# The last feed-forward projection as seven products of halves for sixteen of its twenty-two row tiles

## The chip, the cores and the metric

The kernel runs on one core of a Trainium2 chip. The metric is the device time of one execution in microseconds (us). A profile gives the span from the first to the last instruction of one execution; the execution's time also holds what lies around the span.

## What is computed

Two layers on 512 tokens of width 1024: dilated attention, a gated feed-forward block (SwiGLU), an mLSTM mixer, a second SwiGLU, and a final RMS norm. The change touches the second half of the last SwiGLU and the norm behind it:

```python
def swiglu(xn, w_in, w_out):
    gu = xn @ w_in
    return (jax.nn.silu(gu[..., :D_FF]) * gu[..., D_FF:]) @ w_out      # D_FF = 2816

h = h + swiglu(rms_norm(h, ffn_norm[i]), ffn_w_in[i], ffn_w_out[i])    # i = 1 is the last
return rms_norm(h, final_norm)
```

So the last projection multiplies the hidden values (512 tokens x 2816) by `w_out` (2816 x 1024), adds the residual `h`, and each token's row of 1024 is normalised and written out. All is float32.

## The kernel before

**How float32 is multiplied.** Each operand is split into a rounded value (`_h`, type fp32r, made on ScalarE, ACT) and a residue (`_l`, made on VectorE, DVE, as source minus rounded value). Each float32 product is then three matmuls (`SPLITS`): high by high, high by low, low by high. For a chunk of weights the two instructions are L208 (ACT) and L209 (DVE), both 128x1024.

**Layer 1 of the feed-forward block** is `ffn_in` (its hidden values) and then the block at L1577 on (its projection). `ffn_in` makes the hidden values in eleven tiles `hid[0]` to `hid[10]`, each two row tiles of 128 of the 2816, by 512 tokens. The first three come from `plain`. The other eight already come as seven products of halves each (`products`, L1186, matmuls 256 wide, accumulators `c`, `p` and `u`). While the last of them (named `f1j20`, since it starts at row tile 20) runs, `split_hidden` begins to split the hidden values into `f1hh` (L1254, ACT) and `f1hl` (L1257, DVE), 128x1024 each, in the order of the tiles.

**The projection before.** For each half `n` of the 1024 output features, the loop runs over eleven chunks of `w_out`, each two row tiles by 512 features (`fw_w`, 512 KB, loaded through SyncE's queue, SP, into three buffers and split into `fw_h` and `fw_l`). A chunk is multiplied with the four blocks of 128 tokens (`tb`), 2 x 3 matmuls of 512 features for each (L1620). In the first half, eight groups of four transposes (`hT`, L305) bring `h` from its feature-major form into token-major tiles `ht` on the way. The last three chunks of a half are held back and multiplied block by block, so that one block after the other ends:

```python
            tiles = [(tb, tb, slice(0, 512)) for tb in range(TB)]
            if n == 1:
                tiles[-1:] = [(TB - 1, TB - 1, slice(0, 256)), (TB, TB - 1, slice(256, 512))]
```

The last block of the second half is thus made in two pieces of 256 features, and its matmuls are 256 wide throughout. Behind each block DVE adds the accumulator to `ht` (L1636), ACT squares it with a running sum (`fsq`, L1639), GpSimd (POOL) multiplies it by the gains `gbc` (L1644), and behind the second half of a block come the inverse root (L1648 to L1655), the scaling of both halves (L1657 on ACT, L1659 on DVE) and two output DMAs (L1658, L1660).

**What sets the order.** The code records operations, and a scheduler places each engine's instructions by their dependences and by the order of recording, so an engine's queue is not the order of the source. A tile is one of a few buffers under a tag; the instruction that first writes it waits until the readers of the tile that held the buffer before are done.

Of the kernel before, what the change touches and what calls it, by code (L numbers as in the profile page):

```python
# [11 lines left out]
F32 = mybir.dt.float32  # L12
F32R = mybir.dt.float32r
# [58 lines left out]
def tile_hybrid_dilated_attn_mlstm(  # L72
# [272 lines left out]
    with ExitStack() as actx:  # L345
# [241 lines left out]
        class Values:  # L587
# [15 lines left out]
            def load(self, key, ch, to, add=False):  # L603
                view = to.rearrange("p (k n) -> p k n", k=2)
                if add:
                    nc.gpsimd.dma_start(view, self.source(key, ch), accum_op=ALU.add)
                else:
                    nc.sync.dma_start(view, self.source(key, ch))
# [416 lines left out]
    PLAIN = 6  # L1025
    AHEAD = 2

    def ffn_in(layer, fp, pair, rbc, hook, following):

# [231 lines left out]
        for n, (j, i) in enumerate(todo):  # L1263
            prepare(n + AHEAD)
            if i == 0:
                steps_of = products(j, prepared[j][1])
            steps_of[i]()
            if i % 2:
                advance()
            if n >= len(todo) - 3:  # L1270
                split_hidden()
        while len(parts[0]) < len(hid):
            split_hidden()
        return [[tiles[k // 2][:, k % 2] for k in range(FC)] for tiles in parts], out_weights
# [302 lines left out]
    with ExitStack() as fctx:  # L1577
        fp = pool(fctx, "ffn1")
        wo = ffn_w_out[1]

        def load(ch, n):
            src = wo[ch * 2 * P:(ch + 1) * 2 * P, n * 512:(n + 1) * 512].rearrange("(k p) n -> p k n", p=P)
            return split_weights(src, [P, 2, 512], "fw%d_%d" % (n, ch))
        a, ready = ffn_in(1, fp, pair, rbc, hook, lambda ch: load(ch, 0))
        gbc = fp.tile([P, D], F32, tag="t1", name="gbc")
        nc.gpsimd.dma_start(gbc, final_norm.unsqueeze(0).to_broadcast([P, D]))

        ht = [[None, None] for _ in range(TB)]
        ht_tiles = [fp.tile([P, 4, SEQ], F32, tag="w8", name="ht%d" % i, bufs=2) for i in range(2)]

        def residual(i):
            tb, n = i // 2, i % 2
            tp = ps.tile([P, 512], F32, tag="so"[i % 2], name="hT%d" % i, bufs=2)
            for k in range(4):
                transpose_into(tp, k, h[4 * n + k][:, tb * P:(tb + 1) * P])
            t = ht_tiles[i // 4][:, i % 4]
            nc.scalar.activation(t, tp, AF.Copy)
            ht[tb][n] = t
        NCH = FC // 2
        fss = fp.tile([P, TB, 3], F32, name="fss")  # L1600
        fpre, fv, fr, fa = (fp.tile([P, TB], F32, name="f" + n) for n in ("pre", "v", "r", "a"))
        nc.gpsimd.memset(fss, 0.0)
        nc.gpsimd.tensor_scalar(gbc, gbc, -0.5, None, op0=ALU.mult)
        tail = 3
        for n in range(2):
            acc = ([acc_tile("fin%d" % i) for i in range(3)] + [ps.tile([P, 512], F32, tag="t", name="fin3", bufs=1)]
                   if n == 0 else
                   [ps.tile([P, 512], F32, tag=tg, name="fin4", bufs=2) for tg in ("s", "s", "o", "o")]
                   + [acc_tile("fin5")])


            tiles = [(tb, tb, slice(0, 512)) for tb in range(TB)]
            if n == 1:
                tiles[-1:] = [(TB - 1, TB - 1, slice(0, 256)), (TB, TB - 1, slice(256, 512))]

            def mm(whl, ch, i, tb, cs):
                for k in range(2):
                    kk = 2 * ch + k
                    for a_, b_ in SPLITS:
                        nc.tensor.matmul(acc[i][:, cs], a[a_][kk][:, tb * P:(tb + 1) * P], whl[b_][:, k, cs],  # L1620
                                         start=(kk == 0 and (a_, b_) == SPLITS[0]),
                                         stop=(kk == FC - 1 and (a_, b_) == SPLITS[-1]))

            for ch in range(NCH - tail):
                whl = ready.pop(0) if ready else load(ch, n)
                for t in tiles:
                    mm(whl, ch, *t)
                if n == 0 and 1 <= ch <= TB:
                    residual(2 * ch - 2)
                    residual(2 * ch - 1)  # L1630
            last = [load(ch, n) for ch in range(NCH - tail, NCH)]
            for at, tb, cs in tiles:
                for i in range(tail):
                    mm(last[i], NCH - tail + i, at, tb, cs)
                t = ht[tb][n][:, cs]
                nc.vector.tensor_tensor(t, acc[at][:, cs], t, op=ALU.add)  # L1636
                junk = npl.tile([P, SEQ], F32, tag="sq", name="fsq", bufs=2)
                part = 0 if n == 0 else 1 if cs.stop < 512 else 2
                nc.scalar.activation(junk[:, cs], t, AF.Square, accum_out=fss[:, tb, part:part + 1])  # L1639
                if part == (1 if tb == TB - 1 else 0):  # L1640
                    nc.vector.tensor_tensor(fpre[:, tb:tb + 1], fss[:, tb, 0:1], fss[:, tb, 1:2], op=ALU.add)
                    nc.vector.tensor_scalar(fpre[:, tb:tb + 1], fpre[:, tb:tb + 1], 1.0 / D, EPS,
                                            op0=ALU.mult, op1=ALU.add)
                nc.gpsimd.tensor_tensor(t, t, gbc[:, n * 512 + cs.start:n * 512 + cs.stop], op=ALU.mult)  # L1644
                if n == 1 and cs.stop == 512:

                    v = fv[:, tb:tb + 1]
                    nc.vector.scalar_tensor_tensor(v, fss[:, tb, 2:3], 1.0 / D, fpre[:, tb:tb + 1],  # L1648
                                                   op0=ALU.mult, op1=ALU.add)
                    r = fr[:, tb:tb + 1]  # L1650
                    a2 = fa[:, tb:tb + 1]
                    nc.scalar.activation(r, v, AF.Sqrt)
                    nc.vector.reciprocal(r, r)
                    nc.vector.tensor_scalar(a2, r, v, r, op0=ALU.mult, op1=ALU.mult)
                    nc.vector.scalar_tensor_tensor(r, a2, -3.0, r, op0=ALU.add, op1=ALU.mult)  # L1655
                    t0, t1 = ht[tb]
                    nc.scalar.activation(t0, t0, AF.Copy, scale=r)  # L1657
                    nc.scalar.dma_start(out[tb * P:(tb + 1) * P, 0:512], t0)  # L1658
                    nc.vector.tensor_scalar(t1, t1, r, None, op0=ALU.mult)  # L1659
                    nc.sync.dma_start(out[tb * P:(tb + 1) * P, 512:1024], t1)  # L1660


# [22 lines left out]
```

## Time and profile before

| | us |
|---|---|
| median of three executions | 1433.47 (1430.98 to 1434.05) |
| the profiled execution's own time | 1431.08 |
| its span | 1428.8 |

The page gives busy time by engine, and windows of the span give it by stage. TensorE's matmul unit is PE, its weight loads are PEld. Matmuls overlap in the pipeline, so the duration of a row is longer than the distance between two starts; how much work a stage holds is read from the starts. POOL's DMAs go through a queue of their own (software), SP's and ACT's through the others.

### The profile page before, as it was taken

What the parts mean: (1) busy time and instruction counts of PE and PEld (TensorE: products, weight loads), DVE (VectorE), ACT (ScalarE), POOL (GpSimd) and SP (SyncE); (2) the same over time, 40 slices, a digit from 0 to 9 for tenths busy, and PEclk for the clock granted to TensorE, in tenths of its full rate; (3) what the DMA queues carried; (4) which work ended last, traced back from release to release, by engine and by line L of the source; (5) the groups of instructions that cost most, each with busy time, mean ns of one, the idle gap of its engine ahead of it and who ended that gap; (6) DMA issues with size and microseconds to landing.
All of it is one profiled execution on the core that took longest, in us unless ns stands there. A gap on an engine that the chain in (4) does not pass through costs nothing. (4 is left out here: it accounts for less than half of the span.)

```text
span 1428.8 us, 20252 instructions
## 1 busy us (share of the span) xinstructions
PE 1410.0 (99%) x7968; PEld 1234.9 (86%) x7968; DVE 988.5 (69%) x1697; ACT 621.3 (43%) x1027; POOL 78.1 (5%) x131
## 2 busy tenths in 40 slices
PE   9999999999999999999999999999999999999997
PEld 7788888888888888999988888798888899998886
DVE  7976685966676587777863359987759777786223
ACT  7245522324224443454542234785544344555222
POOL 1014010100001000000000010100000000000101
PEclk9999999999999999999999999999999999999998
DMA  9538353363525333332233333221233233313231
GB/s 297 144 86 210 96 167 121 99 211 98 176 89 165 108 95 111 119 118 80 70 111 97 103 91 89 75 75 50 84 102 101 93 118 119 105 59 119 74 118 59
DMA packets 132182, 160.74 MB, mean 112 GB/s; under 512 B 7092, under 2 KB 112884, under 8 KB 132088
## 3 DMA queue, kind: packets, MB, share of 16 engines
q1 hardware_dynamic: 123696, 135.75, 30.7%
q0 software_dynamic: 6736, 22.59, 6.1%
q8 instruction: 62, 1.02, 0.3%
q10 hardware_dynamic: 1656, 1.12, 0.2%
q14 instruction: 32, 0.26, 0.1%
HBM read 145.28 MB, written 12.06 MB: 110 GB/s over the span
## 5 line engine op out<-in xcount | busy, mean ns | idle before, releaser
L1620 PE MATMUL fin<-fw_h,f1hh 128*128 128x512 f32 (+1 forms) x198 | 72.8, 368 | 0.0
L1620 PE MATMUL fin<-fw_l,f1hh 128*128 128x512 f32 (+1 forms) x198 | 72.5, 366 | 0.0
L1620 PE MATMUL fin<-fw_h,f1hl 128*128 128x512 f32 (+1 forms) x198 | 72.4, 366 | 0.0
L209 DVE TENSOR_TENSOR fw_l<-fw_w,fw_h 128x1024 fp32r<-128x1024 f32 x22 | 27.0, 1233 | 65.5 <-ACT fw_h L208 65.5
L209 DVE TENSOR_TENSOR fo_k_l<-fo_k_w,fo_k_h 128x1024 fp32r<-128x1024 f32 (+1 forms) x24 | 27.2, 1133 | 62.0 <-ACT fo_k_h L208 62.0
L239 PE MATMUL fo<-f0hh,fo_k_h 128*128 128x512 f32 x176 | 68.5, 389 | 0.0
L239 PE MATMUL fo<-f0hl,fo_k_h 128*128 128x512 f32 x176 | 68.5, 389 | 0.0
L239 PE MATMUL fo<-f0hh,fo_k_l 128*128 128x512 f32 x176 | 68.5, 389 | 0.0
L208 ACT ACTIVATE fo_k_h<-fo_k_w 128x1024 fp32r<-128x1024 f32 (+1 forms) x24 | 23.7, 989 | 74.4 <-PE fo L239 74.4
L208 ACT ACTIVATE fw_h<-fw_w 128x1024 fp32r<-128x1024 f32 x22 | 23.3, 1059 | 67.8 <-PE fin L1620 67.8
L1620 PEld LDWEIGHTS fin<-fw_h,f1hl 128*128 128x128 f32 x198 | 37.3, 189 | 6.1
L1620 PEld LDWEIGHTS fin<-fw_l,f1hh 128*128 128x128 f32 x198 | 37.4, 189 | 6.0 <-DVE fw_l L209 0.2
L1620 PEld LDWEIGHTS fin<-fw_h,f1hh 128*128 128x128 f32 x198 | 37.4, 189 | 6.0
L239 PEld LDWEIGHTS fo<-f0hh,fo_k_h 128*128 128x128 f32 x176 | 33.0, 188 | 6.9
L239 PEld LDWEIGHTS fo<-f0hl,fo_k_h 128*128 128x128 f32 x176 | 33.0, 188 | 6.9
L239 PEld LDWEIGHTS fo<-f0hh,fo_k_l 128*128 128x128 f32 x176 | 33.0, 188 | 6.7
L239 PE MATMUL f1j<-n_h,f1j_h 128*128 128x512 f32 x96 | 37.5, 390 | 0.0
L239 PE MATMUL f0j<-n_h,f0j_h 128*128 128x512 f32 x96 | 37.5, 390 | 0.0
L239 PE MATMUL f0j<-n_h,f0j_l 128*128 128x512 f32 x96 | 37.4, 389 | 0.0
L239 PE MATMUL f1j<-n_h,f1j_l 128*128 128x512 f32 x96 | 37.4, 389 | 0.0
L239 PE MATMUL f0j<-n_l,f0j_h 128*128 128x512 f32 x96 | 37.3, 389 | 0.0
L239 PE MATMUL f1j<-n_l,f1j_h 128*128 128x512 f32 x96 | 37.3, 389 | 0.0
(2127 smaller groups left out, 4896.8 us busy)
## 6 DMA issues: line engine op xcount, KB each, us to landing
f0j_w<-in_ffn_w_in_dram SPq DMA_DIRECT2D x28, 512.0 KB, 4.8
f1j_w<-in_ffn_w_in_dram SPq DMA_DIRECT2D x28, 512.0 KB, 3.6
fw_w<-in_ffn_w_out_dram SPq DMA_DIRECT2D x22, 512.0 KB, 3.9
fo_k_w<-in_ffn_w_out_dram SPq DMA_DIRECT2D x20, 512.0 KB, 3.4
awo_k_w<-in_attn_w_out_dram SPq DMA_DIRECT2D x8, 512.0 KB, 4.5
mv_k_w<-in_mlstm_w_in_dram SPq DMA_DIRECT2D x8, 512.0 KB, 3.6
mqk_k_w<-in_mlstm_w_in_dram SPq DMA_DIRECT2D x8, 512.0 KB, 3.8
mo_k_w<-in_mlstm_w_in_dram SPq DMA_DIRECT2D x8, 512.0 KB, 3.6
```

The lines of the kernel that those rows point to most:

```text
L208: nc.scalar.activation(hi[:, :n], raw[:, :n], AF.Copy)
L209: nc.vector.tensor_tensor(lo[:, :n], raw[:, :n], hi[:, :n].bitcast(F32), op=ALU.subtract)
L239: nc.tensor.matmul(acc, whl[a][:, k, m * P:(m + 1) * P], pairs[b][kk], start=(kk == 0 and (a, b) == SPLITS[0]), stop=(kk == nk - 1 and (a, ...
L1620: nc.tensor.matmul(acc[i][:, cs], a[a_][kk][:, tb * P:(tb + 1) * P], whl[b_][:, k, cs], start=(kk == 0 and (a_, b_) == SPLITS[0]), stop=(k ...
```

## The change

The loop over two halves and eleven chunks goes. The first eight hidden tiles (sixteen row tiles) become one unit, halved three ways: the row tiles into K1 (`hid[0..3]`) and K2 (`hid[4..7]`), the tokens into two pairs of blocks, the features into two halves of 512. With `b11`, `b12`, `b21`, `b22` for the hidden values (K half, token half) and `a11`, `a12`, `a21`, `a22` for the weights (feature half, K half), the four results are made from seven products in place of eight: `a11*B11`, `a12*B21`, `s1*T1`, `s2*T2`, `s3*T3`, `s4*B22`, `a22*T4`. The token forms T1 to T4 are made on DVE in place (L1387) and split again (L1346 on ACT, L1348 and L1350 on DVE, 128x512 each). The weight sums are `s1 = a21 + a22`, `s2 = s1 + a11`, `s3 = a11 + a21`, `s4 = s2 + a12`. For `s1`, `s3` and `s4`, POOL's DMAs add a second block of `w_out` onto a tile in SBUF as they land (L1302, twelve of them); DVE makes `s2` (L1335). The other three hidden tiles (six row tiles) are multiplied plainly, `p0` and `p1` for the two feature halves.

The order is written out: 34 items (a product or plain part, and a chunk `c` of it), 28 of 12 matmuls and six of 24, all 512 wide. The weights of an item are prepared two items ahead, and `STEPS` says at which item which token form is made:

```python
HALF_ORDER = (("a11", "B11"), ("a12", "B21"), ("p0", None), ("s1", "T1"), ("s2", "T2"), ("p1", None),
              ("s3", "T3"), ("s4", "B22"), ("a22", "T4"))
```

Accumulators: `c` starts as `a11*B11`; ACT copies it (L1444) into `u`, and `a12*B21` and `p0` go on in `c`, `s2*T2`, `s3*T3` and `a22*T4` in `u`, `s1*T1` and `s4*B22` in `p`. After a product, DVE folds its result into `ht` (L1785). The eight groups of transposes stand behind the first four items. The gains are two tiles of 512, loaded and scaled (L1770) in the middle of the unit. The last two chunks of `a22` run for token blocks 0 and then 1, 512 wide; there is no 256-wide piece any more. The core of the diff:

```diff
-        a, ready = ffn_in(1, fp, pair, rbc, hook, lambda ch: load(ch, 0))
+        unit = Halves(1, fp, wo)
+        ffn_in(1, fp, pair, rbc, hook, unit.prepare, unit)
...
-            if n >= len(todo) - 3:
+            if unit is not None:
+                unit.early(n - len(todo) + len(PRODUCTS))
+            elif n >= len(todo) - 3:
                 split_hidden()
...
+        def load_own(self, c):
+            p, tag = (self.fp, ("op12", "op13", "t1")[c]) if c < 3 else (xp, "x7")
+            self.own[c] = p.tile([P, 1024], F32, tag=tag, name="o%down%d" % (self.layer, c))
+            self.load(self.own[c], 1, c)
+            self.load(self.own[c], 1, 4 + c, True)
...
+        def prepare(self, n):
...
+                raw = self.first[c // 2][:, c % 2] if key == "s3" else self.own[c]
+            self.made[n] = split_chunk((raw, 1024, lambda t: t.rearrange("p (k n) -> p k n", k=2), nm))
+            if key == "s2":
+                self.load(self.own[c], 0, 4 + c, True)
+            if n + 2 < len(self.items) and self.items[n + 2][0] == "s2":
+                c2 = self.items[n + 2][2]
+                first = self.first[c2 // 2][:, c2 % 2]
+                nc.vector.tensor_tensor(self.own[c2], self.own[c2], first, op=ALU.add)
+                self.load(first, 1, c2, True)
...
+                to, x, y, op, sign = {"T1": (b11, b11, b12, ALU.subtract, 1.0), "T2": (b11, b22, b11, ALU.add, -1.0),
+                                      "T3": (b12, b22, b12, ALU.subtract, 1.0),
+                                      "T4": (b21, b11, b21, ALU.subtract, 1.0)}[what]
+                nc.vector.tensor_tensor(to, x, y, op=op)
+                self.split_form(what, i, to, sign)
+
+        EARLY = {2: (("B11", 0),), 3: (("B11", 1),), 4: (("B11", 2),), 5: (("B11", 3),), 6: (("B21", 0), ("B21", 1))}
+        STEPS = {0: (("B21", 2),), 1: (("B21", 3), ("plain", 8)), 2: (("plain", 9),), 3: (("plain", 10),),
...
+                 13: (("T3", 2),), 15: (("T3", 3),), 16: (("B22", 0),), 17: (("B22", 1),),
...
+                    if key == "a11" and last:
+                        banks["u"] = [bank("o", 2) for _ in range(2)]
+                        for t in range(2):
+                            nc.scalar.activation(banks["u"][t], banks["c"][t], AF.Copy)
...
+        def finish(tb, n):
+            t = ht[tb][n]
+            junk = npl.tile([P, SEQ], F32, tag="sq", name="fsq", bufs=2)
+            nc.scalar.activation(junk, t, AF.Square, accum_out=fss[:, tb, n:n + 1])
+            nc.gpsimd.tensor_tensor(t, t, gbc[n], op=ALU.mult)
...
+        def mul(dst, t, okey, c, whl, first, last):
+            for k in range(2):
+                for a, b in SPLITS:
+                    nc.tensor.matmul(dst[t], unit.form(okey, a, 2 * c + k)[:, t * P:(t + 1) * P], whl[b][:, k],
...
+        def after(banks, key, t):
+            if key == "s1":
+                fold(2 + t, 1, banks["p"][t], ALU.subtract)
+            elif key == "s2":
+                fold(2 + t, 0, banks["u"][t])
...
+            elif key == "a22":
+                fold(t, 1, banks["u"][t], ALU.subtract)
+                finish(t, 1)
```

**DVE, where the second product begins.** In the rows below, `o1a12c` is the chunk `c` of `a12` (`_l` its residue), `o1T2_3` and `o1T1_1` residues of token forms, and a row that writes `f1hid` makes a token form in place. Before, from the end of the last hidden tile on:

```order
L1229 TENSOR_TENSOR f1hid10_11517<-f1j20_u_11360,f1j20g1_11452 128x2x256
L1257 TENSOR_TENSOR f1hl5_11575<-f1hid6_10620,f1hh6_11573 128x1024
L209 TENSOR_TENSOR fw0_2_l_11671<-fw0_2_w_11668,fw0_2_h_11670 128x1024
L1257 TENSOR_TENSOR f1hl6_11579<-f1hid7_10845,f1hh7_11577 128x1024
L1257 TENSOR_TENSOR f1hl7_11583<-f1hid8_11070,f1hh8_11581 128x1024
L1257 TENSOR_TENSOR f1hl8_11587<-f1hid9_11295,f1hh9_11585 128x1024
L209 TENSOR_TENSOR fw0_3_l_11713<-fw0_3_w_11710,fw0_3_h_11712 128x1024
L1257 TENSOR_TENSOR f1hl9_11591<-f1hid10_11517,f1hh10_11589 128x1024
L209 TENSOR_TENSOR fw0_4_l_11755<-fw0_4_w_11752,fw0_4_h_11754 128x1024
L209 TENSOR_TENSOR fw0_5_l_11797<-fw0_5_w_11794,fw0_5_h_11796 128x1024
```

Now, from the residue of the second chunk of `a12` to that of the fourth:

```order
L209 TENSOR_TENSOR o1a121_l_11699<-o1a121_w_11696,o1a121_h_11698 128x1024
L1387 TENSOR_TENSOR f1hid2_9596<-f1hid6_10620,f1hid2_9596 128x2x256
L1387 TENSOR_TENSOR f1hid3_9945<-f1hid7_10845,f1hid3_9945 128x2x256
L1387 TENSOR_TENSOR f1hid0_9257<-f1hid4_10170,f1hid0_9257 128x2x256
L1350 SCALAR_TENSOR_TENSOR o1T2_3_11887<-f1hid2_9596,o1T2_2_11886 128x512
L1387 TENSOR_TENSOR f1hid1_9436<-f1hid5_10395,f1hid1_9436 128x2x256
L1387 TENSOR_TENSOR f1hid2_9596<-f1hid6_10620,f1hid2_9596 128x2x256
L1387 TENSOR_TENSOR f1hid3_9945<-f1hid7_10845,f1hid3_9945 128x2x256
L209 TENSOR_TENSOR o1a122_l_11741<-o1a122_w_11738,o1a122_h_11740 128x1024
L1350 SCALAR_TENSOR_TENSOR o1T2_3_11887<-f1hid3_9945,o1T2_2_11886 128x512
L209 TENSOR_TENSOR o1a123_l_11767<-o1a123_w_11764,o1a123_h_11766 128x1024
```

Before, a chunk's residue stood among residues of hidden tiles, and then chunk followed chunk; now seven rows on token forms stand between the second and the third chunk of `a12`.

**DVE at the very end.** `fin4` and `fin5` are the last accumulators before, `o1_o` is `u` now; the number behind `ht` is the block and the half. Before, the last two pieces of the last block:

```order
L1636 TENSOR_TENSOR ht1_11596<-fin4_11999,ht1_11596 128x256
L1655 SCALAR_TENSOR_TENSOR fr_11600<-fa_11601,fr_11600 128x1
L1659 TENSOR_SCALAR ht1_11596<-ht1_11596,fr_11600 128x512
L1641 TENSOR_TENSOR fpre_11598<-fss_11597 128x1
L1642 TENSOR_SCALAR fpre_11598<-fpre_11598 128x1
L1636 TENSOR_TENSOR ht1_11596<-fin5_12000,ht1_11596 128x256
L1648 SCALAR_TENSOR_TENSOR fv_11599<-fss_11597,fpre_11598 128x1
L1653 RECIPROCAL fr_11600<-fr_11600 128x1
L1654 TENSOR_SCALAR fa_11601<-fr_11600,fv_11599 128x1
L1655 SCALAR_TENSOR_TENSOR fr_11600<-fa_11601,fr_11600 128x1
L1659 TENSOR_SCALAR ht1_11596<-ht1_11596,fr_11600 128x512
```

Now, blocks 0 and 1 in the second half:

```order
L1785 TENSOR_TENSOR ht01_11687<-ht01_11687,o1_o_11720 128x512
L1797 SCALAR_TENSOR_TENSOR fv_11569<-fss_11567,fpre_11568 128x1
L1799 RECIPROCAL fr_11570<-fr_11570 128x1
L1800 TENSOR_SCALAR fa_11571<-fr_11570,fv_11569 128x1
L1801 SCALAR_TENSOR_TENSOR fr_11570<-fa_11571,fr_11570 128x1
L1805 TENSOR_SCALAR ht01_11687<-ht01_11687,fr_11570 128x512
L1785 TENSOR_TENSOR ht11_11694<-ht11_11694,o1_o_11721 128x512
L1797 SCALAR_TENSOR_TENSOR fv_11569<-fss_11567,fpre_11568 128x1
L1799 RECIPROCAL fr_11570<-fr_11570 128x1
L1800 TENSOR_SCALAR fa_11571<-fr_11570,fv_11569 128x1
L1801 SCALAR_TENSOR_TENSOR fr_11570<-fa_11571,fr_11570 128x1
L1805 TENSOR_SCALAR ht11_11694<-ht11_11694,fr_11570 128x512
```

The last accumulator was added in a piece of 256 behind rows of an earlier piece; now it is added 512 wide, behind the scaling of the block before it.

**SP, the loads around the start.** `own` and `first` are the tiles in which the weight sums grow. Before:

```order
L1149 DMA f1j20A22_11259<-in_ffn_w_in_dram 128x4x256
L1149 DMA f1j20A12_11260<-in_ffn_w_in_dram 128x4x256
L200 DMA fw0_0_w_11487<-in_ffn_w_out_dram 128x2x512
L200 DMA fw0_1_w_11526<-in_ffn_w_out_dram 128x2x512
L200 DMA fw0_2_w_11668<-in_ffn_w_out_dram 128x2x512
L200 DMA fw0_3_w_11710<-in_ffn_w_out_dram 128x2x512
L200 DMA fw0_4_w_11752<-in_ffn_w_out_dram 128x2x512
L200 DMA fw0_5_w_11794<-in_ffn_w_out_dram 128x2x512
```

Now:

```order
L1149 DMA f1j20A12_11260<-in_ffn_w_in_dram 128x4x256
L1304 DMA o1a110_w_11493<-in_ffn_w_out_dram 128x2x512
L1304 DMA o1own2_11661<-in_ffn_w_out_dram 128x2x512
L1304 DMA o1first2_11823<-in_ffn_w_out_dram 128x2x512 x2
L1304 DMA o1a111_w_11530<-in_ffn_w_out_dram 128x2x512
L1304 DMA o1a112_w_11573<-in_ffn_w_out_dram 128x2x512
L1304 DMA o1a113_w_11614<-in_ffn_w_out_dram 128x2x512
L1304 DMA o1a120_w_11655<-in_ffn_w_out_dram 128x2x512
L1304 DMA o1own0_11579<-in_ffn_w_out_dram 128x2x512
L1304 DMA o1own1_11620<-in_ffn_w_out_dram 128x2x512
L1304 DMA o1a121_w_11696<-in_ffn_w_out_dram 128x2x512
L1304 DMA o1a122_w_11738<-in_ffn_w_out_dram 128x2x512
```

Five loads of tiles for the sums now stand among the loads of the first chunks (and two, `o1first0`, just ahead of these rows), each waiting for its own buffer.

More of the change, by code (lines that the diff above doesn't have):

```diff
@@ L1026, in tile_hybrid_dilated_attn_mlstm, with ffn_in @@
     AHEAD = 2
-    def ffn_in(layer, fp, pair, rbc, hook, following):
+    def ffn_in(layer, fp, pair, rbc, hook, following, unit=None):
         wi = ffn_w_in[layer]
@@ L1597, in residual, with gains_in @@
             nc.scalar.activation(t, tp, AF.Copy)
-            ht[tb][n] = t
-        NCH = FC // 2
-        fss = fp.tile([P, TB, 3], F32, name="fss")
+        def gains_in():
+            for n in range(2):
+                t = hp.tile([P, SEQ], F32, tag="h", name="gbc%d" % n, bufs=KC + 1)
+                nc.gpsimd.dma_start(t, final_norm[n * 512:(n + 1) * 512].unsqueeze(0).to_broadcast([P, 512]))
+                nc.gpsimd.tensor_scalar(t, t, -0.5, None, op0=ALU.mult)
+                gbc.append(t)
@@ L1601, in tile_hybrid_dilated_attn_mlstm, with also @@
+        def also(n):
+            if n < 4:
+                for i in (2 * n, 2 * n + 1):
+                    residual(i % TB, i // TB)
+            elif n == 6:
+                gains_in()
+        fss = fp.tile([P, TB, 2], F32, name="fss")
         fpre, fv, fr, fa = (fp.tile([P, TB], F32, name="f" + n) for n in ("pre", "v", "r", "a"))
         nc.gpsimd.memset(fss, 0.0)
[L1603 to L1616, printed above, removed]
-                for k in range(2):
[L1618 to L1660, printed above, removed]
@@ new lines, in mul, with mul_plain @@
+        def mul(dst, t, okey, c, whl, first, last):
+            for k in range(2):
+                for a, b in SPLITS:
+                    nc.tensor.matmul(dst[t], unit.form(okey, a, 2 * c + k)[:, t * P:(t + 1) * P], whl[b][:, k],
+                                     start=(first and k == 0 and (a, b) == SPLITS[0]),
+                                     stop=(last and k == 1 and (a, b) == SPLITS[-1]), skip_group_check=True)
+        rest = {}
+        def mul_plain(banks, key, c, whl, fresh, last):
+            n = int(key[1])
+            if fresh:
+                rest[n] = ([*banks["c"], unit.bank("acc", 3), unit.bank("t", 1)] if n == 0 else
+                           [unit.bank("acc", 3) for _ in range(3)] + [unit.bank("t", 1)])
+            for tb in range(TB):
+                for k in range(2):
+                    for a, b in SPLITS:
+                        nc.tensor.matmul(rest[n][tb], unit.plain[c][a][k][:, tb * P:(tb + 1) * P], whl[b][:, k],
+                                         start=(fresh and (n == 1 or tb >= 2) and k == 0 and (a, b) == SPLITS[0]),
+                                         stop=(last and k == 1 and (a, b) == SPLITS[-1]), skip_group_check=True)
+                if last:
+                    fold(tb, n, rest[n][tb])
+                    if n == 0 and tb < 2:
+                        finish(tb, 0)
@@ L1664 @@
+        unit.run((2, mul, mul_plain, after), also)
 _INS = ['x', 'positions', 'attn_norm', 'attn_w_in', 'attn_w_out', 'mlstm_norm', 'mlstm_w_in',
```

158 lines of the change are left out of this document (148 added, 10 removed), and 3 rows, old and new, of the table STEPS.

## The prediction

> **What bounds the kernel now.** I read the page first, then windows of the last stages, then PE's waits, then the chain of waits, then DVE's and POOL's timelines around the start of the projection and at the end.
>
> ```profile
> span 1428.8 us, 20252 instructions
> PE 1410.0 (99%) x7968; PEld 1234.9 (86%) x7968; DVE 988.5 (69%) x1697; ACT 621.3 (43%) x1027; POOL 78.1 (5%) x131
> ```
>
> PE is busy all the time, but busy rows overlap, so this alone doesn't say that PE is the limit. The windows of the projection (1294 to 1419) show each engine's share there, first PE, PEld, DVE, ACT and POOL:
>
> ```profile
> 1294.00:1326.00 32.00, 32.00 (x161) 26.92 (x160) 14.68 (x15) 12.24 (x16) 0.00 (x0) 1.00 0.36 117
> 1326.00:1360.00 34.00, 34.00 (x151) 28.05 (x150) 11.06 (x17) 9.23 (x15) 3.87 (x3) 1.00 0.23 66
> 1360.00:1419.00 59.00, 59.00 (x322) 51.26 (x321) 17.22 (x30) 15.75 (x25) 6.05 (x5) 1.00 0.26 87
> ```
>
> DVE works 43 of these 125 us and ACT 37, the DMA engines a quarter to a third of the time, and the granted clock is 1.00. All of PE's waits from 1060 us on, in one row, and the chain of waits around the projection's start and end (start, us, what) say the same: matmul follows matmul.
>
> ```profile
> PE f1j_u L1186 <- DVE f1j20v L1192: 0.2, 1, 0.2
> ```
>
> ```profile
> 1291.57 3.11 PE f1j_u L1186 x24
> 1294.67 10.91 PE fin L1620 x48
> 1305.59 0.88 PE hT L305 x8
> 1306.47 5.47 PE fin L1620 x24
> ...
> 1404.99 14.07 PE fin L1620 x79
> 1419.07 0.02 issue
> 1419.09 0.43 DVE ht L1636
> ...
> 1419.55 0.52 ACT fsq L1639 x2
> ...
> 1421.28 0.72 ACT ht L1657
> ```
>
> So fewer matmuls here are worth their distance from start to start, as long as DVE and ACT, which get more to do, don't fall behind.
>
> **The matmuls.** The chain's 48 in 10.91 us give 0.2273 us for one of 512. Two starts of the 256-wide ones give 0.12 us, and the groups of the window give the counts (one of three alike each):
>
> ```profile
> 1379.79 0.28 PE L1620 MATMUL fin<-fw_h,f1hh 128*128 128x256 f32 x1
> 1379.91 0.28 PE L1620 MATMUL fin<-fw_l,f1hh 128*128 128x256 f32 x1
> ```
>
> ```profile
> L1620 PE MATMUL fin<-fw_h,f1hh 128*128 128x512 f32 x154 | 60.4, 392 | 0.0
> L1620 PE MATMUL fin<-fw_h,f1hh 128*128 128x256 f32 x44 | 12.4, 282 | 0.0
> ```
>
> Before: 462 x 0.2273 + 132 x 0.12 + 4 x 0.88 for the transposes = 105.0 + 15.8 + 3.5 = 124.3 us; the chain has 1294.67 to 1419.07, 124.4. After: 28 items of 12 and six of 24 are 480 matmuls, 109.1, and the same transposes, 3.5: 112.6. That is **-11.8 us**: 48 matmuls saved by the eighth product, 10.9, and 0.9 since 132 pieces of 256 become 66 of 512. The 0.2 us of PE's only wait should go too, as DVE has less ahead of it there (below): **-0.2**.
>
> **DVE in the first products.** An item of 12 matmuls lasts 2.73 us, where a chunk took 5.46. In that time DVE owes a residue of weights and much of a token form. The rows on DVE, back to back and beside a POOL row:
>
> ```profile
> 1285.16 2.06 DVE L209 TENSOR_TENSOR f1j20S_l<-f1j20A,f1j20S_h 128x1024 fp32r<-128x1024 f32 x1
> 1287.14 2.54 DVE L1257 TENSOR_TENSOR f1hl<-f1hid,f1hh 128x1024 fp32r<-128x1024 f32 x2
> 1289.60 1.22 DVE L209 TENSOR_TENSOR f1j20A_l<-f1j20A,f1j20A_h 128x1024 fp32r<-128x1024 f32 x1
> ...
> 1294.20 1.22 DVE L209 TENSOR_TENSOR fw_l<-fw_w,fw_h 128x1024 fp32r<-128x1024 f32 x1
> 1295.34 0.68 DVE L1225 TENSOR_TENSOR f1hid<-f1j20v,f1j20g 128x512 f32<-128x512 f32 x1
> 1295.94 0.68 DVE L1229 TENSOR_TENSOR f1hid<-f1j_u,f1j20g 128x512 f32<-128x512 f32 x1
> ...
> 1298.81 3.73 DVE L1257 TENSOR_TENSOR f1hl<-f1hid,f1hh 128x1024 fp32r<-128x1024 f32 x3
> ```
>
> ```profile
> L227 DVE SCALAR_TENSOR_TENSOR yo_l<-y,halfgain,yo_h 128x512 fp32r<-128x512 f32 x8 | 5.8, 745 | 0.0
> ```
>
> ```profile
> 1284.85 3.04 POOL L1603 TENSOR_SCALAR gbc<-gbc 128x1024 f32<-128x1024 f32 x1 [3.24 <-DMA gbc<-in_final_norm_dram]
> ```
>
> From start to start, 1.14 us for 1024 and 0.60 for 512 where nothing waits (1294.20 to 1295.34 to 1295.94); full durations are 1.22 and 0.68. Now the race. The residue of the last hidden product's weights ends at 1290.82. Ahead of it five `f1hl` rows go (5.7 us) and eight of 512 come (4.8), and the POOL row that stretched one to 2.06 moves away (0.8): 1289.1. From there to the residue of `a122` (third chunk of the second product) the new queue has 34 rows: seven of 1024, 24 of 512, three of the 0.745 kind. Back to back 8.0 + 14.4 + 2.2 = 24.6 us, so 1313.7. PE needs it after four items with transposes, 4 x (2.73 + 0.88), and two without: 1294.67 + 14.4 + 5.5 = 1314.6. Spare: 0.9. With full durations it is 27.1 us and 1316.2: a stall of 1.6. The next seven rows, to the first chunk of `p0`, take 5.4 and end at 1319.1, needed at 1320.0; behind that six plain chunks' time, 5.46 each, is ample. The gains' scaling, now two POOL rows of 512, comes here, as their buffers are those of `h` behind the last transposes (1309 at the earliest); beside it one DVE row grew by 0.84. So 0 to 2.9 us (2.1 late by full durations, plus 0.8). I take **+0.5**, near the low end, since the rows nearest to it are the back-to-back ones.
>
> **The rest of the added work lies beside PE.** Over the 112 us DVE has 34 residues (39 us), 28 token residues and 16 forms of 512 (27), four sums (5), folds and plain residues (15): 86 us, no bound as a whole. ACT's copy of `c` into `u` and its neighbours in the queue:
>
> ```profile
> 1257.74 0.58 ACT L1198 ACTIVATE f1j_u<-f1j_c 128x512 f32<-128x512 f32 x1
> ```
>
> The second accumulator is written again 0.88 + 1.36 us after its last matmul (transposes, six matmuls of the other), so 0.58, even behind another row of that size, is covered. The loads, plain ones of a chunk and those of POOL's queue that add onto a tile (issue on POOL, then landing):
>
> ```profile
> DMA to landing us min/median/max: 3.7/3.9/4.7
> ```
>
> ```profile
> L606 POOL DMA_DIRECT2D v12w<-in_attn_w_in_dram x4: 1260/1262/1752, 111.4 to 130.9; - x4
> DMA to landing us min/median/max: 5.9/7.0/8.8
> ```
>
> A chunk's buffer comes free with the residue three items (8 us) ahead of its own: a load of 4.7 is hidden, also behind the two `own` loads that SP must pass once the last hidden product frees their buffers (1294.6). The sums: `s1` is first needed at 1320.0 + 16.4 = 1336.4, its load can start at 1294.6, so 4.7 + 1.8 + 8.8 leaves over 20 us. `s3` is needed at 1374.6, and its adds can go out behind DVE's sums `s2`, by 1344 at the latest; `s4` ten us later than `s3`, its adds from 1354 on. All free while these covers hold.
>
> **The end.** The last residue, of `a22`'s fourth chunk, stands on DVE and ACT behind the finish of blocks 2 and 3, with the table load for the root on ACT. The rows (min, median, max; a minimum here is the 256-wide form):
>
> ```profile
> L1652 ACT ACT_TABLE_LOAD x1 | 1.3, 1283 | 0.0
> ```
>
> ```profile
> L1636 DVE TENSOR_TENSOR ht<-fin,ht x9: 417/690/692, 1345.9 to 1419.1; 128x512 f32<-128x512 f32 x7, 128x256 f32<-128x256 f32 x2
> L1639 ACT ACTIVATE fsq<-ht x9: 416/632/633, 1346.7 to 1419.5; 128x512 f32<-128x512 f32 x7, 128x256 f32<-128x256 f32 x2
> L1644 POOL TENSOR_TENSOR ht<-ht,gbc x9: 722/1293/1388, 1347.6 to 1420.1; 128x512 f32<-128x512 f32 x7, 128x256 f32<-128x256 f32 x2
> L1659 DVE TENSOR_SCALAR ht<-ht,fr x4: 486/486/488, 1410.4 to 1421.3; 128x512 f32<-128x512 f32 x4
> ```
>
> ```profile
> 1422.03 0.34 ACTq L1658 DMA_DIRECT2D out_dram<-ht  x1
> ```
>
> After `s4` come a fold (0.7), a square (0.8 with its read of the sum), the table load (1.3), some six small rows (1.1), two scalings (1.0) and the residue (1.2): 6.1 us, less the 1.0 that this overlaps. PE has 2 x 2.73 + 1.36 = 6.8 us of `a22` before it needs that residue. Spare 0.7 to 1.7; 0 to 0.5 lost, taken as **+0.2**.
>
> Behind the last matmul, the last output DMA was issued 2.96 us later (1419.07 to 1422.03). Now the add is 0.27 longer, the square 0.21, POOL's row 0.57 longer, of which 0.15 sticks out behind the root's small rows. And DVE comes late: block 0 ends 2.73 ahead, its add, square, POOL row and scaling take 0.7 + 0.85 + 1.3 + 0.5 = 3.4, and the last add stands behind that scaling: 0.7. Together **+1.3**, between 0.5 (were DVE free) and 1.6 (the slowest POOL row twice).
>
> **Sum.** -11.8 - 0.2 + 0.5 + 0.2 + 1.3 = -10.0 us. Against the profiled execution's 1431.08 that is 1421.1 (its span 1428.8 and 2.3 around it); the median of the runs shown lies 2.4 higher, at 1433.47, and from it the forecast is **1423.5 us**.
>
> **The rivals.**
>
> *DVE falls behind and stays behind.* The three `f1hl` rows from 1298.81 took 3.73, that is full durations without overlap. If the whole dense stretch goes so, and ACT's roundings, which DVE waits for, add theirs, PE stalls at the third and fourth chunk of `a12` and at `p0`, and again where sums `s2` and folds meet: 3 to 6 us in all. Against it: the rows at 1294 to 1296 keep 1.14 and 0.60, and PE's own stall gives DVE time back. 1426.5 to 1429.5.
>
> *POOL's rows hold DVE altogether.* In the trace a DVE row beside the 3.04 us POOL row took 2.06 in place of 1.22, and the next two (1287.14, 2.54 for two) no more than usual, though POOL worked to 1287.89. If instead a row of DVE waits for the whole of a POOL row, the gains' scaling costs 3.0 in the tight stretch, with 0.9 spare, and each POOL row beside the end 0.5 more: -7.4, so 1426. The Trainium skill has this as a rule (SBUF — State Buffer, "SBUF: two separate sides"): the pair of ports that both engines share is locked for a whole instruction, and a DVE instruction with two SBUF inputs blocks against a GpSimd one that reads SBUF. The trace agrees that there is a cost, with 0.84 us of 3.04, not that it is the whole; by the rule the sum would be -7.4.
>
> *The weight sums land late, and the kernel gets slower.* Twelve DMAs of POOL's queue wait for a plain load or for DVE, in order, behind one another and behind the gains. Slack is least at `s3`: adds from 1345 on, one every 1.8 us, landing by 1361, needed at 1374.6, so 14 us. From there each microsecond costs one, and past 24 us late the gain of 10.0 is used up: landings of over 30 us where the longest of eight was 8.8. That they passed beside a DVE at work speaks against it.
>
> *The change doesn't save what it says.* If matmuls take longer from start to start with operands in other buffers, or the clock falls, 480 of them at 0.25 us cost 10.9 more, and nothing is won. All 512-wide matmuls of the chain keep 0.227 to 0.228, whatever their tiles, and the windows show a clock of 1.00.
>
> **How the numbers follow.** The sum with stalls of up to 3 us: 0.63. DVE behind: 0.20. POOL's lock: 0.07. Sums late: 0.04. No gain from the matmuls: 0.04. A little better than all this: 0.02. The range starts at no stall and a tail of 0.5 against the lowest run, 1430.98 - 11.5 = 1419.5, rounded down to 1419, and ends where DVE behind ends, 1429: it leaves out late sums, slow matmuls and the last of DVE behind, some 0.1 to 0.2. A change below 0.2% (2.9 us) can't be told from none: faster 0.91, same 0.04, slower 0.05.
>
> **What would show it.** Right: 480 rows of L1811 and L1824, 0.227 us apart, in about 113 to 114 us from the first to the last; PE's waits there below 1.5 us, on residues of `a122`, `a123` or `p00` if anywhere, and one on the last of `a22`; the last output issued 4 to 4.5 us behind the last matmul. Wrong: waits of PE on DVE that add up to several microseconds in the first ten items or among `s1` and `s2`; ACT or DVE waiting for DMAs of `own` or `first`; DVE rows of 2 us and more beside POOL's.

## The result, and the profile after

The changed kernel took 1420.65 us (median of five, 1418.90 to 1422.58) against 1432.53 for the kernel before: ratio 0.9918, 95% interval 0.9905 to 0.9932. In a later comparison it was 1421.29 against 1431.72, ratio 0.9930 (0.9916 to 0.9943). So it is 10 to 12 us faster; the forecast was 10.0 less, 1423.5 us.

The top of the page after, and PE's waits from 1060 us on (line, releaser, us in total, times, longest):

```profile
span 1418.6 us, 20164 instructions
PE 1399.9 (99%) x7854; PEld 1221.9 (86%) x7854; DVE 1030.6 (73%) x1756; ACT 641.0 (45%) x1059; POOL 95.6 (7%) x146
```

```profile
PE hT L305 <- ACT ht L1764: 0.6, 1, 0.6
PE o_acc L1824 <- DVE o1p_l L209: 0.5, 1, 0.5
```

PE is still at 99%, and 10.1 us less busy. The stages ahead of the last projection hold the same instructions, yet their end scatters: its first matmul stood at 1293.94 to 1299.09 us in the fourteen profiles of this study. From the first matmul of the mLSTM's output projection to that point the distance is 271.94 before and 271.52 to 271.55 in the two profiles of the changed kernel, so the scatter lies ahead of it. I therefore compare stretches, not spans, each from start to start:

| stretch, us | before | forecast | changed | changed, second profile |
|---|---|---|---|---|
| mLSTM output projection to the last projection | 271.94 | -0.2 | 271.52 | 271.55 |
| its first matmul to its last | 124.26 | 113.2 | 115.27 | 113.15 |
| last matmul to the last output's issue | 3.26 | +1.3 | 4.61 | 4.61 |
| that issue to the end of the span | 6.82 | same | 4.78 | 4.78 |
| sum | 406.28 | -10.0 | 396.18 | 394.09 |

The chain of waits of the changed kernel (start, us, what), where it leaves PE, where it comes back, and the end:

```profile
1291.22 2.88 PE f1j_u L1186 x24
1294.10 2.77 PE o_acc L1811 x12
...
1296.93 1.07 ACT o1a_h L208
...
1305.76 10.11 DMA o1a_w<-in_ffn_w_out_dram
...
1315.98 1.07 ACT o1a_h L208
...
1320.70 1.15 DVE o1p_l L209
...
1321.89 4.23 PE o_acc L1824 x17
```

```profile
1349.32 10.89 PE o_o L1811 x48
...
1409.84 0.49 DVE ht L1805
1410.33 0.61 DVE ht L1785
...
1413.07 0.72 ACT ht L1803
```

Before, this chain was PE alone from 1291.57 to the last fold. Now it runs for 25 us, from 1296.93 to 1321.89, through ACT, DVE and one load that took 10.1 us to land. From `s1` (1338.28) on, all is as forecast: 48 matmuls in 10.88 or 10.89 us, 0.2267 each. Of the 115.27 us, 44.34 lie ahead of `s1`, where 168 matmuls at 0.2267 and 3.5 of transposes make 41.6: 2.7 lost. PE's two listed waits are 1.1 of it; the rest is spread over starts that came late by less. The windows name the suspect (last two columns: the DMA engines' share and GB/s):

```profile
1294.00:1309.00 15.00, 14.36 (x76) 11.49 (x76) 12.74 (x18) 10.36 (x17) 2.43 (x2) 1.00 0.91 286
1309.00:1320.00 11.00, 10.97 (x51) 8.63 (x50) 9.16 (x14) 7.53 (x12) 2.34 (x3) 1.00 1.00 244
```

In the kernel before, the share from 1294 to 1326 was 0.36.

### The profile page after: what moved, and what is told of

Same layout as the page of the kernel before. It is cut to its first block, busy times and chain, and to the rows that moved or that the text cites. A ratio compares the mean times of both kernels' runs of the same rounds, so it can differ in the third digit from the quotient of the medians.

```text
span 1418.6 us, 20164 instructions
## 1 busy us (share of the span) xinstructions
PE 1399.9 (99%) x7854; PEld 1221.9 (86%) x7854; DVE 1030.6 (73%) x1756; ACT 641.0 (45%) x1059; POOL 95.6 (7%) x146
## 5 line engine op out<-in xcount | busy, mean ns | idle before, releaser
L1302 POOL DMA_DIRECT2D o1own<-in_ffn_w_out_dram x8 | 9.7, 1226 | 287.7 <-DVE o1B L1348 259.8
L524 DVE TENSOR_TENSOR rot<-rot,sinr 32x1024 f32<-32x1024 f32 x24 | 28.9, 1205 | 0.0
L239 PE MATMUL mo<-n_h,mo_k_h 128*128 128x512 f32 x64 | 25.4, 397 | 0.0
L239 PE MATMUL mo<-n_h,mo_k_l 128*128 128x512 f32 x64 | 25.2, 394 | 0.0
L239 PE MATMUL mo<-n_l,mo_k_h 128*128 128x512 f32 x64 | 25.2, 393 | 0.0
L239 PE MATMUL mqk<-n_h,mqk_k_h 128*128 128x512 f32 x64 | 25.1, 393 | 0.0
L239 PE MATMUL awo<-ao_h,awo_k_h 128*128 128x512 f32 x64 | 25.1, 392 | 0.0
```

Source lines behind the costliest of these rows:

```text
L239: nc.tensor.matmul(acc, whl[a][:, k, m * P:(m + 1) * P], pairs[b][kk], start=(kk == 0 and (a, b) == SPLITS[0]), stop=(kk == nk - 1 and (a, ...
L524: nc.vector.tensor_tensor(sh, sh, sinr.unsqueeze(1).to_broadcast([R, 2, SEQ]), op=ALU.mult)
L1302: nc.gpsimd.dma_start(view, self.source(col, ch), accum_op=ALU.add)
```

## Experiment 1: what costs the time ahead of `s1`

Two edits, alone and together, and a third that takes transfers away. The first puts the loads of `own` and `first` behind the weight chunks on SP's queue (`own` at items 4 to 7, `first` at 8 to 11):

```diff
-                if n < 4:
-                    self.load_own(n) if n < 3 else None
-                elif n == 4:
-                    self.load_own(3)
-                if 5 <= n < 9:
-                    self.load_first(n - 5)
+                with tc.issue_after(last_on(mybir.EngineType.SP)):
+                    if 4 <= n < 8:
+                        self.load_own(n - 4)
+                    if 8 <= n < 12:
+                        self.load_first(n - 8)
```

> All 480 matmuls and all sums stay; only the loads of the sums' chunks (own, first) stand behind the weight chunks of the first products on SP's queue. Measured: time from the first matmul of the projection (L1811) to the first of product s1. It is 44.3 us in the changed kernel, against 168 matmuls at 0.2267 plus 3.5 for the 32 transposes = 41.6, so 2.7 us are lost there. Theory T (transfers: the 16 DMA engines are full from 1294 to 1336 us and chunks land late): the wait of 0.5 us in p0 and the slow a123 go, 43.0 to 43.4. Theory Q (queues: forms that are needed 30 us later stand in ACT's and DVE's order ahead of the copies and residues that PE waits for): 44.1 to 44.5. Theory N (neither; the loss is in PE's own starts): 44.3. The time moves by as much, 1 us or 0.1%.

The second holds the scheduler from moving splits and forms ahead of what is written before them:

```diff
-                for what, i in self.STEPS.get(n, ()):
-                    self.step(what, i)
+                with tc.issue_after(last_on(mybir.EngineType.DVE)), tc.issue_after(last_on(mybir.EngineType.Activation)):
+                    [self.step(what, i) for what, i in self.STEPS.get(n, ())]
```

> The same instructions; the splits and token forms of the steps stand on DVE and ACT behind all that is written before them, so a form no longer comes ahead of a chunk's rounding, its residue, or the copies of hT. Loads as in the changed kernel. First matmul of the projection to the first of s1 (44.3 us now, 41.6 with no loss): theory Q: the wait of hT (0.6), of the copy of c to u (0.3 to 0.5) and the slow residues of a12 go, 42.3 to 43.0, and the time falls by 1.3 to 2 us. Theory T: the late chunks stay, and with them what they cost, 43.9 to 44.4. Theory N: 44.3. A form that now comes too late for its own product would show as a new wait of PE behind 1338 us (none is expected: T2's forms end some 5 us ahead of s2).

> The edits of the two runs before together. First matmul of the projection to the first of s1: theory Q alone: as with late forms only (42.3 to 43.0). Theory T alone: as with spread loads only (43.0 to 43.4). Both causes in turn: 41.7 to 42.2, near the sum of matmuls, and 2.2 to 2.6 us off the time. Theory N: 44.3.

```diff
             if add:
-                nc.gpsimd.dma_start(view, self.source(col, ch), accum_op=ALU.add)
+                pass
```

> Leaves out the twelve accumulating DMAs (8 KB per partition row and 512 KB each), so the sums s1, s3 and s4 lack their second terms and s2 two of its four. First matmul of the projection to the first of s1: theory T: six to eight fewer loads before 1336 us, so the share of the DMA engines falls from 1.00 to about 0.75, chunks land in 4 to 5 us, 43.0 to 43.4. Theory Q: 44.1 to 44.5, since ACT and DVE keep their order. Theory N: 44.3. From s1 on nothing changes by any theory (70.9 us to the last matmul).

(Each of these transfers is 512 KB, so 4 KB and not 8 for each partition.) Measured (medians, against 1432.67 before in that comparison):

| run | us | ratio (95%) | first matmul to `s1` | `s1` to the last |
|---|---|---|---|---|
| loads spread | 1419.49 | 0.9914 (0.9899 to 0.9929) | 41.89 | 70.98 |
| forms late | 1420.73 | 0.9918 (0.9903 to 0.9933) | 41.91 | 71.18 |
| both | 1426.03 | 0.9957 (0.9942 to 0.9971) | 41.89 | 76.71 |
| no adding DMAs | 1423.09 | 0.9938 (0.9920 to 0.9956) | 41.89 | 71.05 |

Neither theory fits: each expected its own cure to bring back a part and the other none. Each edit alone brings back 2.4 of the 2.7, and PE has no wait left in the stretch. So the loss needs both: loads that land late, and a dense order on ACT and DVE that has no room for them. The rounding of `a112` shows it. Relative to the first matmul it starts at +2.99 us in the changed kernel and at +0.13 with spread loads:

```profile
1294.82 1.06 ACT L208 ACTIVATE o1a_h<-o1a_w 128x1024 fp32r<-128x1024 f32 x1 [0.18 <-ACT o1T L1346]
```

Behind that rounding in ACT's order come the copies of `hT`, and in DVE's order the forms of T1 and the residues of `a12`. With late forms it starts at +1.56, with the DMA engines as busy as before (0.96 and 0.97 in the two windows), and nothing dense stands behind it. What is read here is the stretch: the times of spread loads and late forms, 0.9914 and 0.9918, can't be told from the changed kernel's own 0.9918, and experiment 4 shows that its loss is not the same in each execution.

Both edits together fail for a new reason. Now the sums stand behind late loads and behind forms that DVE makes when they are due, and PE waits for residues of the sums in the middle of `s1`, 3.6 us in these two rows, while the stretch is 5.8 longer:

```profile
PE o_s L1811 <- DVE o1s_l L209: 2.9, 1, 2.9
PE o_s L1811 <- ACT o1s_h L208: 0.7, 1, 0.7
```

That is the rival "the weight sums land late", at `s1` rather than `s3`.

The kernel without adding DMAs gives its 2.4 us back elsewhere: its projection began 1.7 us later by the scatter ahead, and from its last output's issue to the end of the span it took 7.9 us where the changed kernel took 4.8. The second part is a row of POOL's that ends the span; it is read with the prediction's terms below.

## Experiment 2: is the gain the number of matmuls?

The first try ran the products of `s4` twice with the finish of blocks 2 and 3 behind each:

```diff
-                    for u in range(units):
+                    for u in [u for u in range(units) for _ in range(1 + (key == "s4"))]:
```

> The products of s4 are formed twice (48 more 512-wide matmuls, 528 in all, as many as before the change; the output then holds s4's product twice). Theory M (the gain is the 48 matmuls, each at the cadence of the rows): s4 takes 21.76 us in place of 10.88, the first matmul of s1 to the last of the projection 81.8 in place of 70.9, and the time rises by 10.9 us to within 1 us of the kernel before (less 1.7: the pieces of 256 columns and what the stage before gained, plus the longer end). Theory O (part of the gain comes from other things that the change does: fewer evictions, a shorter way into the projection): the time rises by 10.9 as well, but stays more than 2.5 us below the kernel before.

It took 1440.68 us, ratio 1.0057 (1.0042 to 1.0072), some 9 us more than either theory allowed. The trace tells why: `s1` to the last matmul is 81.69 us as expected, but the last output is issued 10.70 us behind the last matmul in place of 4.61, and the span ends 7.4 us later behind that matmul, since two blocks are folded, squared and sent out twice. The edit was too wide and its time tells nothing of the question. The second try repeats the matmuls alone:

```diff
-                        for c_ in chunks:
+                        for c_ in chunks * (1 + (key == "s4")):
```

> The matmuls of s4 alone twice (the earlier run also folded and finished blocks 2 and 3 twice, which made its end longer). 528 matmuls; the output holds s4's product twice. First matmul of s1 to the last: 70.9 + 48 x 0.2267 = 81.8 us; last output's issue 4.6 behind it as in the changed kernel; time 10.9 above the changed kernel's in the same call, by theory M. By theory O (part of the gain is not the number of matmuls) this kernel stays more than 2.5 us below the kernel before; by M alone it is 0.5 to 1.5 below it (the pieces of 256 columns, 1.05 us on PE in the run with the block unsplit, the 0.2 of the stage before, less 1.6 at the end, plus what is lost ahead of s1).

```profile
1390.86 21.76 PE o_s L1811 x96
```

96 matmuls take 21.76, `s1` to the last 81.78, and the end is 4.60. The time is 1431.69 against 1431.72 before: ratio 1.0003 (0.9994 to 1.0012). With as many matmuls as before, nothing of the gain is left, so theory O falls: the gain is the 48 matmuls. The repeated matmuls use weights that are already there, so no load, rounding or residue comes with them. Theory M put this kernel 0.5 to 1.5 below the one before; the interval, some 1.5 us either way, doesn't tell that from equal.

The 256-wide pieces, undone in the kernel before:

```diff
-                tiles[-1:] = [(TB - 1, TB - 1, slice(0, 256)), (TB, TB - 1, slice(256, 512))]
+                pass
```

> The kernel before with its last block of rows not cut in halves of 256 columns: 66 matmuls of 512 in place of 132 of 256. The prediction's terms: 0.9 us less on PE (132 x 0.1202 = 15.9 against 66 x 0.2273 = 15.0), and behind the last matmul a fold, a square and a scaling of 512 columns in place of 256, 0.5 to 0.7 more from the last matmul to the last output's issue. Net -0.4 to -0.2: no difference that can be timed; the two terms are read from the trace. If the pieces cost nothing on PE: the projection's matmuls last 124.4 as now, and the time is 0.6 longer.

```profile
1330.04 92.54 PE fin L1620 x408
```

Before, the same stretch of the chain was `1325.48 93.59 PE fin L1620 x474`: 66 matmuls fewer and 1.05 us less (forecast 0.9). From the last matmul to the last output's issue it took 4.07 us in place of 3.26. From the projection's first matmul to that issue it is 127.15 us in place of 127.52, so -0.4 together, and the ratio is 1.0003 (0.9993 to 1.0012), as expected.

## Experiment 3: the end

`scale_late` keeps the scaling of a block's second half, and its output DMA, for later: after the residue of `a223` for blocks 2 and 3, after the fold of block 1 for block 0.

```diff
-            nc.vector.tensor_scalar(t1, t1, r, None, op0=ALU.mult)
-            (nc.sync if tb < 2 else nc.gpsimd).dma_start(out[tb * P:(tb + 1) * P, 512:1024], t1)
+            late.append((nc.vector.tensor_scalar, (t1, t1, r, None), dict(op0=ALU.mult)))
+            late.append(((nc.sync if tb < 2 else nc.gpsimd).dma_start, (out[tb * P:(tb + 1) * P, 512:1024], t1), {}))
...
-                fold(t, 1, banks["u"][t], ALU.subtract)
+                fold(t, 1, banks["u"][t], ALU.subtract); t and scale_late()
```

> The changed kernel; the scalings of the second halves (a DVE row of 0.44 to 0.49 each, and their output DMAs) stand behind what DVE has to do next for PE: those of blocks 2 and 3 behind the residue of a223, that of block 0 behind the fold of block 1. Theory Q (in-order DVE): the wait of PE on a223 goes (first matmul of s1 to the last 70.93 to 70.5), the last output is issued 4.1 us behind the start of the last matmul in place of 4.61, and the time falls by 0.9. Theory C (the end is the chain of small operations, whatever stands between): 4.61 stays, and only the 0.4 before it goes. Theory N: the wait of a223 is its rounding on ACT or its load: nothing changes.

> The loads of the first run of these experiments (own and first behind the weight chunks) together with the late scalings. If the two add: first matmul of the projection to the first of s1 41.9 (44.34 in the changed kernel), from there to the last 70.5 (70.93), to the last output's issue 4.1 (4.61): 3.4 us less than the changed kernel, a ratio to the kernel before of 0.989 to 0.990. If spreading the loads only moved the loss, its s1 sums come late now and then, and the ratio stays at 0.9918.

Alone it took 1420.71 (ratio 0.9915, 0.9901 to 0.9930), with spread loads 1419.04 (0.9906, 0.9889 to 0.9922). `s1` to the last matmul fell from 70.93 to 70.70 in both, so half of the wait for `a223` went. The end stayed: 4.57 in place of 4.61. DVE's and ACT's rows of the second run show what took the place of DVE's order:

```profile
1408.97 0.68 DVE L1794 TENSOR_TENSOR ht<-ht,o_o 128x512 f32<-128x512 f32 x1
```

```profile
1409.08 0.72 ACT L1812 ACTIVATE ht<-ht,fr 128x512 f32<-128x512 f32 x1 [0.98 <-DVE fr L1810]
1409.83 0.34 ACTq L1813 DMA_DIRECT2D out_dram<-ht  x1
1410.21 0.63 ACT L1799 ACTIVATE fsq<-ht 128x512 f32<-128x512 f32 x1 [0.41 <-DVE ht L1786]
```

Block 1's fold is done at 1409.6, but its square waits until 1410.21 for block 0's scaling and output issue on ACT. Two queues held the same place; freeing DVE's alone changes nothing. So ACT's half was moved too, behind block 1's root, with spread loads and with late forms:

```diff
             t0, t1 = ht[tb]
+            if tb == 1:
+                o0, r0 = ht[0][0], fr[:, 0:1]
+                with tc.issue_after(last_on(mybir.EngineType.Activation)):
+                    nc.scalar.activation(o0, o0, AF.Copy, scale=r0)
+                nc.sync.dma_start(out[0:P, 0:512], o0)
+            if tb > 0:
...
```

> Spread loads and late scalings, and of block 0 the ScalarE scaling of the first half too, behind block 1's square root, its output issued by SP. In the run with the DVE scaling alone moved, block 1's fold began 0.46 us behind the start of the last matmul, but its square waited until 1.70 behind it for block 0's scaling (0.72) and DMA issue (0.34) on ACT. Theory Q (in-order ACT): the square starts 1.1 behind, and the last output is issued 4.0 to 4.2 behind the start of the last matmul in place of 4.57 (block 0's scaling may now delay block 1's by 0.1). Theory C (a chain of block 1 alone): 4.57. Stretches as in the run before it: 41.9 and 70.7. Ratio to before 0.989 to 0.990.

> The same end with late forms in place of spread loads. If late forms free PE of the loads' chance (theory Q): 41.9 again to s1, 70.7 to 71.0 from there, 4.0 to 4.2 at the end, ratio 0.989 to 0.990. If the 41.9 of the first run with late forms was a lucky one: 42.3 to 44.3 to s1.

With spread loads: 1417.72 us, ratio 0.9902 (0.9889 to 0.9916); 41.90 to `s1`, 70.70 from there, 4.03 at the end, each as theory Q had it. Here the square starts 0.03 us behind block 1's fold, and ahead of the end of DVE's late scaling (1408.77), so before it was ACT's own order that held it and not the DVE row that the trace names:

```profile
1408.40 0.63 ACT L1799 ACTIVATE fsq<-ht 128x512 f32<-128x512 f32 x1 [1.58 <-DVE ht L1794]
```

With late forms: 1419.44, ratio 0.9913 (0.9900 to 0.9927); 41.89, 71.33 and 4.03. Late forms cost 0.6 us somewhere behind `s1`, which I did not follow up. The first of the two is the best version: in the same comparison the changed kernel had 0.9930 (0.9916 to 0.9943).

## Experiment 4: the changed kernel once more

> The changed kernel once more, since in two later profiles with its order of loads and forms (the product twice, the late scalings) the stretch from the first matmul of the projection to the first of s1 was 42.3 and 42.7 us, against 44.34 in its own profile. Theory L (the loss is a chance meeting of late loads with the order of ACT and DVE, not a fixed cost): anywhere from 41.9 to 44.5, most likely 42.3 to 43.5, and its times scatter by as much. Theory F (a fixed cost of 2.4 to 2.7 us): 44.2 to 44.5. Time 1419 to 1422 by both; ratio to the kernel before 0.991 to 0.993.

42.22 us to `s1`, with no wait of PE. Five profiles have the changed kernel's order ahead of `s1`: 44.34, 42.22, 42.34 (finish twice), 42.72 (scaling late) and 44.43 (`s4` twice). Theory F falls, and theory L's bounds hold: the loss over 41.6 is 0.6 to 1.1 in three and 2.7 to 2.8 in two, while the seven profiles with an edit of experiment 1 in them have 41.89 to 41.91. In the second profile the rounding of `a112` starts at +1.71, and its wait has a load's name:

```profile
1298.57 1.06 ACT L208 ACTIVATE o1a_h<-o1a_w 128x1024 fp32r<-128x1024 f32 x1 [1.58 <-DMA o1a_w<-in_ffn_w_out_dram]
```

The load of `a112` was issued 5.88 us ahead of the first matmul in both (at 1288.06 in the first profile, 1290.97 in the second). In the second the wait for it ended at 1298.49, after 7.5 us. In the first the trace names PE for the rounding's wait, but the matmuls that held the buffer had ended 2.8 us before, and SP's queue, which waited for the same load, was released with ACT at 1296.85, so the load took 8.8 us:

```profile
SPq L1304 <- DMA o1a_w<-in_ffn_w_out_dram: 0.4, 1, 0.4
```

The other profile with a long loss has the same pair of releases, 8.8 us behind the issue. With spread loads this load took 3.9. So in the changed kernel's order the loss goes with the landing of this one load: 0.6 to 1.1 at 7.5 to 7.8 us and 2.7 to 2.8 at 8.8. With late forms the load took 7.7 and PE has no wait. Why it lands later in one execution than in another stays open.

## Why the prediction was right, and where it was not

- **Matmuls, -11.8.** Right, and shown apart: 10.88 per product, 1.05 for the pieces, and no gain with 528 matmuls.
- **PE's only wait, -0.2.** It went: the hidden product's last 24 took 3.11 and now 2.88.
- **DVE in the first products, +0.5 (0 to 2.9).** The size holds in the bounds, at 0.6 to 1.1 and 2.7 to 2.8, but the step ahead of it failed: "a load of 4.7 is hidden". The price came from a stage where the DMA engines were busy for a third of the time. Here the chunk loads, those of `own` and `first`, and the adding DMAs meet, the engines are at 0.91 to 1.00, and chunks landed in 7.5 to 10.1 us: 8.8 (`a112`), 8.4 (`a122`) and 10.1 (`a123`) in the first profile. The race of 34 DVE rows with 0.9 to spare was near the truth, since with spread loads the residue of `a122` ended 1.8 ahead of its first use; but it counted DVE's work alone: a late load delays ACT's rounding, and DVE and the `hT` copies behind it, by more than that spare.
- **Last residue, +0.2 (0 to 0.5).** 70.93 against 70.5 for 311 distances of 0.2267: 0.4. Half of it was the scaling ahead of it on DVE.
- **The end, +1.3 (0.5 to 1.6).** 1.35, so the size was right. The reason was half right: "the last add stands behind that scaling" is true of DVE, but ACT held the same place.
- **Not in the sum:** 2.0 us behind the last output's issue, 6.82 before and 4.78 after. No engine computes there, but all wait for POOL's DRAIN, the row at the end of its instructions (duration in ns, min, median and max; before, then changed):

```profile
L1681 POOLq DRAIN  x3: 46/97/7958, 1420.1 to 1428.6; - x3
```

```profile
L1867 POOLq DRAIN  x3: 46/98/6087, 1411.7 to 1418.3; - x3
```

The long one ended at 1428.05 before and at 1417.81 now. SP's, which stands behind the landing of the last output, ended at 1424.95 and 1416.70, so the last output did not set the end of the span. POOL did: its last multiplication by the gains ended 2.08 us behind the start of the last matmul before and 3.81 now, and the DRAIN another 7.20 and 4.79 behind that. The prediction's term for the end followed the output and left POOL's end out. Ten of the eleven profiles with the change's twelve adding DMAs have 4.79 (the other is the one with the finish twice), and the three without them 7.20 (the kernel before), 7.21 (without pieces) and 7.45 (no adding DMAs). So the shorter DRAIN goes with these DMAs; why it is shorter is open. It made good what was lost ahead of `s1` in the first profile, so that -10.0 came so near there is luck.
- **The base.** The forecast stood on a median of 1433.47, where later ones of the kernel before were 1431.7 to 1432.7: 0.8 to 1.8 of the 2.9 by which 1423.5 was too high.
- **The rivals.** DVE did not fall behind as a whole: nothing is lost among `s1` and `s2`. Late sums came only with both edits. Matmuls kept their distance. "POOL's rows hold DVE altogether" was right in its mechanism for some rows and wrong in its price; see the last section.

## What to carry to other kernels

A landing time read from a stage with little DMA traffic is no price for a stage to which the change adds most of its transfers: add up the bytes by window first. Where two in-order queues (ACT's and DVE's here, at the end and in the first products) both hold the same step, relieving one can show nothing, and a combination of two cures can open a third wait, so try them singly and together. When stages ahead scatter by more than the effect, compare the stretch between two instructions of the trace. And ask which engine ends last: here the span hung on POOL's end and not on the last output.

## What the runs showed of the hardware

A POOL row with two inputs in SBUF held a DVE row with two inputs until its own end. At 1400 us (POOL, then DVE; the pair of DVE rows, then min, median and max of the four of that line):

```profile
1400.27 2.98 POOL L1791 TENSOR_TENSOR ht<-ht,gbc 128x512 f32<-128x512 f32 x2 [7.90 <-ACT fsq L1790]
```

```profile
1400.76 1.31 DVE L1797 SCALAR_TENSOR_TENSOR fv<-fss,fpre 128x1 f32<-128x1 f32 x2
```

```profile
L1797 DVE SCALAR_TENSOR_TENSOR fv<-fss,fpre x4: 146/159/1245, 1400.8 to 1411.7; 128x1 f32<-128x1 f32 x4
```

One column took 1.245 us in place of 0.15, and ended as the first POOL row did (1.713 us long, so 1401.98). The small row on the last chain does the same, ending with the POOL row at 1413.0:

```profile
1411.76 1.26 POOL L1791 TENSOR_TENSOR ht<-ht,gbc 128x512 f32<-128x512 f32 x1 [2.04 <-ACT fsq L1790]
```

```profile
1412.65 0.39 DVE L1801 SCALAR_TENSOR_TENSOR fr<-fa,fr 128x1 f32<-128x1 f32 x1
```

That is what the Trainium skill says (SBUF — State Buffer, "SBUF: two separate sides"): the shared ports are locked for an instruction, and a DVE instruction with two SBUF inputs waits for a GpSimd one that reads SBUF. By this trace it holds beside POOL's TENSOR_TENSOR. Beside POOL's TENSOR_SCALAR it does not hold as a whole: in the kernel before, the DVE row of 2.06 us ended at 1287.22, and the POOL row at 1287.89. In the kernel without adding DMAs it was POOL's rows that grew: the two of the gains took 10.59 us where the changed kernel's take 3.11 (both below), while most DVE rows of two inputs beside them kept their 1.22 and 0.69.

```profile
1314.59 10.59 POOL L1770 TENSOR_SCALAR gbc<-gbc 128x512 f32<-128x512 f32 x2 [3.25 <-DMA gbc<-in_final_norm_dram]
```

On the path the lock cost 0.2 us at the end, and not the 2.6 by which the rival's sum differs, since the gains' scaling fell beside `p0`, where DVE was waiting for ACT:

```profile
1324.50 3.11 POOL L1770 TENSOR_SCALAR gbc<-gbc 128x512 f32<-128x512 f32 x2 [7.58 <-DMA gbc<-in_final_norm_dram]
```

```profile
1327.37 1.22 DVE L209 TENSOR_TENSOR o1p_l<-o1p_w,o1p_h 128x1024 fp32r<-128x1024 f32 x1 [2.59 <-ACT o1p_h L208]
```

POOL's queue, 6.3 of its 7.34 MB here from the adding DMAs, keeps the DMA engines busy longer for its bytes than SP's plain loads do. From 1270 to 1420 us (MB, share of the sixteen engines):

```profile
q1 hardware_dynamic: 6695, 12.86, 26.2%
q0 software_dynamic: 3584, 7.34, 25.7%
```

That is 2.0% for each MB on SP's queue and 3.5% on POOL's, and the adding DMAs landed in 5.8, 7.7 and 13.2 us (min, median, max). Whether the adding or the queue makes the difference is not shown. I had priced them by their landing only.
